# Token norms by one GpSimd power, and the rotary and gate multiplications on VectorE, in a two-layer hybrid encoder

## The chip, the cores and the metric

The kernel runs on one core of one Trainium2 chip. The metric is the device time of one execution in microseconds (us), taken as the median of several executions. One further execution is profiled; the trace and all its views come from that one.

## What is computed

A trunk of two layers works on 512 tokens of width 1024, in float32. Each layer does this, and a last RMSNorm follows:

```python
h = rms_norm(x, g_mix);  z = h @ w_in            # q, k, v, xb, gb
q, k = partial_rope(q), partial_rope(k)          # 16 of 64 columns rotate
o = softmax(q1 k1) - lam * softmax(q2 k2), @ v   # 4 heads
o = rms_norm(o, subln) * (1 - lam_init)          # per head
c = centred_dwconv(xb)                           # 4 taps
for d in (forward, backward):                    # RG-LRU
    r, i = sigmoid(c @ w_r), sigmoid(c @ w_i)
    a = exp(-8 r softplus(-A));  u = c * i * sqrt(1 - a*a);  h_d = scan(a, u)
r = rms_norm((h_f + h_b) * gelu(gb), norm_g)
x += concat(o, r) @ w_out
x += cross_attention(rms_norm(x, g_xq), rms_norm(mem, g_mem))   # 4 heads, 256 memory tokens
x += relu(rms_norm(x, g_mlp) @ w1)**2 @ w2
```

`rms_norm(x, g)` is `x * rsqrt(mean(x*x) + 1e-6) * g`.

## The kernel before

**Layout and products.** The residual x stands transposed, as eight tiles of 128 channels by 512 tokens. Each weight block of 128x1024 is loaded by DMA, split by ScalarE into a rounded part (`whi`) and by VectorE into the remainder (`wlo`), and each product is three matmuls of float32r parts. The results lie in PSUM, in three banks called `mm` and five called `at`; VectorE and ScalarE bring them out.

**Norms.** The factor of a token is not multiplied into x ahead of a product, but into its result. A `Norm` adds up squares; `rstd` sums them over partitions by four matmuls with ones, makes the mean square `ms` (128x4: four token blocks) on VectorE and calls `rsqrt_small`, which builds the reciprocal root by a bit trick and three Newton steps: ten VectorE instructions on 128x4, each needing the one before. Four TensorE transposes (`bcast`) then spread the factor over the partitions. There are 18 such calls: one for each of the three token norms of a layer (six), the last norm, the memory norm, the recurrent norm of each layer (two) and the norm of each attention head (eight, `Head.norm`, where three VectorE instructions make `ms` and one multiplies after).

**Rotary and gates.** `qk_one` takes q or k of one head out of PSUM: a shuffle and a multiplication with `Cr` on VectorE, a multiplication of the shuffled tile with `Sr` on GpSimd, a sum on VectorE, then the split. There are 16 of these. `lru_gates` computes sigmoids for two channel blocks and two directions; the input gate of each is multiplied with the conv's output on GpSimd, 16 in all. GpSimd also does the small zeroing at the edges of the conv's tile `xb` (two columns) and two of the last eight output multiplications.

**Order of the work.** The program is recorded as operations with a key (TensorE time at which they are due, less a lead), and `Plan.schedule` makes one order for all queues: each engine in turn takes the operation that can start first by the plan's own durations, and among those that can start at the same moment the one of smallest key:

```python
            lim = smin + self.LOOK      # LOOK = 0.0
            return min(((k, i, s) for s, k, i in best if s <= lim))
```

An operation becomes ready 0.2 us (`LAT`) after one on another engine, and on VectorE 0.127 us (`OWN`) after one on its own. The durations come from `Plan.cost`. The chip then runs each engine's list strictly in that order, waiting on semaphores. `FILL` and `ORDER` say how much projection, recurrence and memory work is recorded between the 16 attention steps of a layer. All of them are issued from line 412, so the rows are told apart by tile names: `s` is every small column tile, `b` every 128x512 tile, `c_ident` and `c_ones` the constants of the transposes and sums.

Of the kernel before, what the change touches and what calls it, by code (L numbers as in the profile page):

```python
# [11 lines left out]
F32 = mybir.dt.float32  # L12
F32R = mybir.dt.float32r
I32 = mybir.dt.int32
AF = mybir.ActivationFunctionType
ALU = mybir.AluOpType
AX = mybir.AxisListType

P = 128
# [131 lines left out]
class Plan:  # L151
# [43 lines left out]
    def cost(self, eng, m, a, k):  # L195
        out = a[0] if a else k["out"]
        n = 1
        for d in out.shape[1:]:
            n *= d
        if eng == "pe":  # L200
            if m == "transpose":
                return 0.109
            f32 = a[1].root.dtype == F32
            if n < 64:
                return 0.224
            return n * 0.00176 if f32 else max(0.114, n * 0.000456)
        if m == "dma_start":
            return 0.06
        if eng == "act":
            t = 0.093 + n * 0.000833  # L210
            t += 0.093 * sum(isinstance(k.get(x), _View) for x in ("scale", "bias", "accum_out"))
            return t
        if eng == "dve":
            if m == "tensor_reduce":
                n = 512
            if m == "tensor_scalar_mul":
                return 0.066 + n * 0.0007
            ap = m == "scalar_tensor_tensor" and isinstance(a[2], _View)
            return 0.067 + n * 0.00105 + 0.06 * ap
        if eng == "pool":  # L220
            return 0.1 + n * (0.0022 if m != "memset" else 0.001)
        return 0.06
# [192 lines left out]
def trunk(tc, ctx, xT, memT, pos, W, par, outT):  # L415
# [10 lines left out]
    V, A, G, PE, SP = (plan.engine(e) for e in ("dve", "act", "pool", "pe", "sp"))  # L426

    def C(shape, dt, name):
        return plan.tile("c_" + name, shape, dt)

    def R():
        return plan.tile("b", [P, S], F32R)

    def T():
        return plan.tile("b", [P, S], F32)

    def SM(n):
        return plan.tile("s", [P, n], F32)

    def MM():  # L440
        return plan.tile("mm", [P, S], F32)
# [4 lines left out]
    def b(v):  # L446
        return v.bitcast(F32)


    def split(dst_hi, dst_lo, src):  # L450
        A.activation(dst_hi, src, AF.Copy)
        V.tensor_tensor(dst_lo, src, b(dst_hi), op=ALU.subtract)
# [19 lines left out]
    def weight(l, t):  # L472
        raw = pre.pop(t, None) if l == 0 else None
        first = raw is not None
        if raw is None:
            raw = raw_weight(l, t)
        hi = plan.tile("whi", [P, 1024], F32R)
        lo = plan.tile("wlo", [P, 1024], F32R)
        with plan.ahead(SPLIT_AHEAD):
            for cs in (slice(0, 512), slice(512, 1024)) if first else (slice(0, 1024),):  # L480
                split(hi[:, cs], lo[:, cs], raw[:, cs])
        return hi, lo

    def gemm_fm(l, t, xs, out, order=range(KD)):

        hi, lo = weight(l, t)
        for i, k in enumerate(order):
            xh, xl = xs[k]
            wh = hi[:, k * P:(k + 1) * P]
            with plan.group():  # L490
                PE.matmul(out, wh, xh, start=(i == 0), stop=False)
                PE.matmul(out, wh, xl, start=False, stop=False)
                PE.matmul(out, lo[:, k * P:(k + 1) * P], xh, start=False, stop=(i == KD - 1))

    def rsqrt_small(ms, n):

        y = SM(n)
        V.tensor_scalar(y.bitcast(I32), ms.bitcast(I32), -0.5, 1597463007.0,
                        op0=ALU.mult, op1=ALU.add)
        for _ in range(3):  # L500
            t = SM(n)
            V.tensor_tensor(t, y, y, op=ALU.mult)
            V.scalar_tensor_tensor(t, t, -0.5, ms, op0=ALU.mult, op1=ALU.mult)
            V.scalar_tensor_tensor(y, t, 1.5, y, op0=ALU.add, op1=ALU.mult)
        return y

    def bcast(col, ncol, out):
# [17 lines left out]
    def pc(l, name, i):  # L525
        o = l * NPL + PC[name] + i
        return prm[:, o:o + 1]
# [4 lines left out]
                    pattern=[[-1, P]], channel_multiplier=1)  # L532
    ones = C([P, P], F32, "ones")
    G.memset(ones, 1.0)

    class Norm:

# [12 lines left out]
        def rstd(self, width, ncol):  # L550
            st = AT()
            with plan.group():
                for c in range(ncol):
                    cs = slice(c * P, (c + 1) * P)
                    PE.matmul(st[:, c:c + 1], self.acc[:, cs], ones[:, 0:1], start=True, stop=True)
            ms = SM(ncol)
            V.tensor_scalar(ms, st[:, :ncol], 1.0 / width, EPS, op0=ALU.mult, op1=ALU.add)
            return rsqrt_small(ms, ncol)
# [66 lines left out]
    def rope_tables(sn, cs, rt):  # L625

        Ct, St = T(), T()
        G.memset(St, 0.0)
        Cv = Ct.split_free(4, 2, 64)
        Sv = St.split_free(4, 2, 64)  # L630
        rb8 = rt.unsqueeze(2).to_broadcast([P, 4, 8])
        rb48 = rt.unsqueeze(2).to_broadcast([P, 4, 48])
        for j in range(2):
            V.tensor_tensor(Cv[:, :, j, 0:8], cs, rb8, op=ALU.mult)
            V.tensor_copy(Cv[:, :, j, 8:16], Cv[:, :, j, 0:8])
            V.tensor_copy(Cv[:, :, j, 16:64], rb48)
            V.tensor_tensor(Sv[:, :, j, 8:16], sn, rb8, op=ALU.mult)
            V.tensor_scalar_mul(Sv[:, :, j, 0:8], Sv[:, :, j, 8:16], -1.0)
        out = []
        for src, tag in ((Ct, "Cr"), (St, "Sr")):  # L640
            p_ = AT()
            with plan.group():
                for c in range(4):
                    PE.transpose(p_[:, c * P:(c + 1) * P], src[:, c * P:(c + 1) * P], ident)
            dst = plan.tile(tag, [P, S], F32)
            A.activation(dst, p_, AF.Copy)
            out.append(dst)
        return out
# [68 lines left out]
    def lru_gates(l, pr, conv, neg, posi):  # L717

        gh, gl = weight(l, T_G + pr)
        gs = {}  # L720
        for c2 in range(2):
            c = 2 * pr + c2
            cc, ch, cl = conv[c]
            for d in range(2):
                for q in range(2):
                    pm = MM()
                    o = (4 * c2 + 2 * d + q) * P
                    with plan.group():
                        PE.matmul(pm, gh[:, o:o + P], ch, start=True, stop=False)
                        PE.matmul(pm, gh[:, o:o + P], cl, start=False, stop=False)  # L730
                        PE.matmul(pm, gl[:, o:o + P], ch, start=False, stop=True)
                    t = T()
                    A.activation(t, pm, AF.Sigmoid, bias=pc(l, "b_i" if q else "b_r", d * 4 + c))
                    if q:
                        G.tensor_tensor(t, cc, t, op=ALU.mult)
                    gs[c2, d, q] = t
        av = {}
        for c2 in range(2):
            for d in range(2):
                r = gs[c2, d, 0]  # L740
                col = l * 8 + d * 4 + 2 * pr + c2
                a, a2 = T(), T()
                A.activation(a, r, AF.Exp, scale=neg[:, col:col + 1])
                A.activation(r, r, AF.Tanh, scale=posi[:, col:col + 1])
                A.activation(a2, a, AF.Square)
                V.scalar_tensor_tensor(r, a2, 1.0, r, op0=ALU.add, op1=ALU.mult)
                av[c2, d] = a
        return gs, av
# [49 lines left out]
    def qk_one(l, t, xs, Cr, Sr, scale):  # L798
        pm = MM()
        gemm_fm(l, t, xs, pm)  # L800
        sh, q = T(), T()
        V.stream_shuffle(sh, pm, SHUF)
        V.tensor_tensor(q, pm, Cr, op=ALU.mult)
        G.tensor_tensor(sh, sh, Sr, op=ALU.mult)
        V.tensor_tensor(q, q, sh, op=ALU.add)
        hi, lo = R(), R()
        if scale is None:
            split(hi, lo, q)
        else:
            A.activation(hi, q, AF.Copy, scale=scale)  # L810
            V.scalar_tensor_tensor(lo, q, scale, b(hi), op0=ALU.mult, op1=ALU.subtract)
        return hi, lo
# [399 lines left out]
    for l in range(DEPTH):  # L1212
# [8 lines left out]
        Cr, Sr = rope_tables(sn, cs, rt)  # L1221
# [221 lines left out]
```

## Time and profile before

| | us |
|---|---|
| median of 3 runs | 1533.76 (1530.17 to 1539.23) |
| the profiled execution | 1536.88 |
| its span, first to last instruction | 1535.1 |
| TensorE busy | 1476.1 |
| VectorE busy | 1183.5 |
| ScalarE busy | 727.1 |
| GpSimd busy | 54.1 |

The busy times come from the profile of that one execution, and a busy TensorE is not a TensorE at full rate: matmul ends are modelled. The trace was read for its mean granted TensorE clock too, 0.978 of full speed over the span. Layer 0 takes the first half of the span, layer 1 the second; in each, attention and recurrence come first, then cross-attention, then the MLP.

### The profile page before, as it was taken

The numbers are of one execution on the slowest core, as the hardware profiler recorded it, in microseconds if no ns is written. First come the engines' busy times: TensorE is split into PE (matmuls) and PEld (weight loads), VectorE is DVE, ScalarE is ACT, GpSimd is POOL, SyncE is SP. The second block draws the span as 40 slices with busy tenths as digits, with TensorE's granted clock in tenths as the row PEclk, the third lists the DMA queues.
The fourth block names the chain that finished last, engine by engine and source line by source line (L and its number), as shares of the span: only waits on it lengthen the run. The fifth ranks groups of instructions, "written<-read, shape, count | busy, mean of one in ns | idle before, by whom it ended". The sixth has DMA issues, their size and how long they took to land.

```text
span 1535.1 us, 20895 instructions
## 1 busy us (share of the span) xinstructions
PE 1476.1 (96%) x8038; PEld 1242.4 (81%) x8038; DVE 1183.5 (77%) x2107; ACT 727.1 (47%) x1099; POOL 54.1 (4%) x59
## 2 busy tenths in 40 slices
PE   8979999999999999999999799999999999999996
PEld 6757788888889889898977577888888898988985
DVE  7899886655589696979868876865656887969696
ACT  5587664444334343434535875553443433434243
POOL 0031000000000000000001310000000000000000
PEclk9989999999999999999999987999999999999998
DMA  5322342311222323222242213422112323232321
GB/s 194 97 82 78 129 138 82 110 69 56 96 96 83 110 84 122 98 97 97 87 134 81 85 57 110 144 101 96 55 69 82 110 84 107 86 110 83 116 88 58
DMA packets 45107, 148.24 MB, mean 97 GB/s; under 512 B 5584, under 2 KB 5712, under 8 KB 45008
## 3 DMA queue, kind: packets, MB, share of 16 engines
q1 hardware_dynamic: 44864, 146.65, 28.0%
q8 instruction: 63, 1.03, 0.3%
q14 instruction: 36, 0.29, 0.1%
q10 hardware_dynamic: 144, 0.26, 0.0%
HBM read 136.41 MB, written 2.10 MB: 90 GB/s over the span
## 4 chain that ended last, share of the span: by engine, by line
PE 85%; DVE 10%; issue 2%; DMA 1%; ACT 1%; SPq 0%; DVEq 0%; ACTq 0%
PE mm L412 65%; PE at L412 20%; DVE b L412 6%; DVE wlo L412 2%; DVE pt L412 1%; DVE s L412 1%; ACT b L412 1%; DMA b<-b 0%; DVE c_x L412 0%; DMA wraw<-in_W 0%; DMA c_x<-in_xT 0%; DMA wraw<-in_memT 0%; SPq L412 0%; ACT whi L412 0%; ACT Cr L412 0%
## 5 line engine op out<-in xcount | busy, mean ns | idle before, releaser
L412 PE MATMUL mm<-b,whi 128*128 128x512 f32 (+1 forms) x3648 | 991.3, 359 | 13.0 <-ACT b L412 6.2
L412 PEld LDWEIGHTS mm<-b,whi 128*128 128x128 f32 x3648 | 638.5, 190 | 126.3 <-ACT b L412 8.6
L412 PE MATMUL mm<-b,wlo 128*128 128x512 f32 (+1 forms) x1824 | 651.0, 357 | 8.0 <-DVE wlo L412 8.0
L412 ACT ACTIVATE whi<-wraw 128x1024 fp32r<-128x1024 f32 (+1 forms) x223 | 233.7, 1049 | 372.6 <-issue 168.3
L412 PEld LDWEIGHTS mm<-b,wlo 128*128 128x128 f32 x1824 | 345.8, 190 | 64.7 <-DVE wlo L412 10.0
L412 DVE TENSOR_TENSOR wlo<-wraw,whi 128x1024 fp32r<-128x1024 f32 (+1 forms) x223 | 277.1, 1243 | 37.2 <-ACT whi L412 36.9
L412 DVE TENSOR_TENSOR b<-b,b 128x512 fp32r<-128x512 f32 (+3 forms) x374 | 219.2, 602 | 15.6 <-ACT b L412 13.3
L412 ACT ACTIVATE b<-b 128x256 fp32r<-128x256 f32 (+2 forms) x224 | 130.3, 596 | 151.9 <-DVE b L412 151.3
L412 DVE TENSOR_TENSOR c_x<-c_x,mm 128x256 f32<-128x256 f32 (+1 forms) x160 | 73.8, 472 | 73.0 <-PE mm L412 71.6
L412 ACT ACTIVATE whi<-pt 128x1024 fp32r<-128x1024 f32 x64 | 67.9, 1061 | 101.6 <-PE mm L412 75.5
L412 PE MATMUL at<-b,whi 128*128 128x256 f32 x512 | 91.8, 278 | 0.0
L412 DVE TENSOR_TENSOR b<-mm,rb 128x512 f32<-128x512 f32 x72 | 49.5, 687 | 53.2 <-PE mm L412 52.5
L412 PE MATMUL at<-b,b 128*128 128x256 f32 (+1 forms) x320 | 83.9, 371 | 3.1 <-DVE b L412 2.2
L412 ACT ACTIVATE b<-at,s 128x512 f32<-128x512 f32 (+2 forms) x100 | 61.0, 614 | 41.9 <-DVE s L412 41.4
L412 DVE TENSOR_TENSOR wlo<-pt,whi 128x1024 fp32r<-128x1024 f32 x64 | 78.2, 1221 | 0.6 <-ACT whi L412 0.3
L412 DVE TENSOR_REDUCE s<-at 128x1 f32<-128x512 f32 (+1 forms) x80 | 54.4, 688 | 31.3 <-PE at L412 31.3
L412 PEld LDWEIGHTS at<-b,whi 128*128 128x128 f32 x512 | 77.6, 188 | 0.0
L412 PEld LDWEIGHTS at<-b,b 128*128 128x128 f32 x320 | 50.1, 195 | 30.9 <-issue 22.6
L412 PE MATMUL at<-b,wlo 128*128 128x256 f32 x256 | 71.1, 278 | 0.0
L412 PE MATMUL at<-pt,b 128*128 128x256 f32 (+1 forms) x288 | 53.1, 332 | 4.2 <-ACT pt L412 2.9
L412 PEld LDWEIGHTS at<-pt,b 128*128 128x128 f32 x288 | 45.3, 200 | 12.2 <-ACT pt L412 3.9
L412 DVE TENSOR_TENSOR c_x<-c_x,at 128x256 f32<-128x256 f32 x96 | 40.1, 419 | 18.1 <-PE at L412 17.7
(124 smaller groups left out, 1311.4 us busy)
## 6 DMA issues: line engine op xcount, KB each, us to landing
wraw<-in_W SPq DMA_DIRECT2D x249, 512.0 KB, 3.2
b<-b SPq DMA_DIRECT2D x64, 128.0 KB, 2.4
wraw<-in_memT SPq DMA_DIRECT2D x4, 512.0 KB, 3.9
out_T<-b SPq DMA_DIRECT2D x8, 256.0 KB, 2.6
c_x<-in_xT SPq DMA_DIRECT2D x7, 256.0 KB, 5.5
wraw<-in_W SPq DMA_DIRECT2D x6, 256.0 KB, 5.5
c_x<-in_xT ACTq DMA_DIRECT2D x1, 256.0 KB, 3.3
c_prm<-in_par SPq DMA_DIRECT2D x1, 89.0 KB, 3.2
```

The lines of the kernel that those rows point to most:

```text
L412: getattr(self.engines[op.eng], m)(*a, **k)
```

## The change

`rsqrt_small` becomes one GpSimd instruction, `ms` to the power of minus one half, with a constant tile of exponents; the multiplications in `qk_one` and in the input gates go from GpSimd to VectorE; and the plan books every GpSimd operation of up to four columns at 1.0 us. That booking holds for the powers and for the zeroing of two columns alike. The order of all queues is made anew from these durations.

```diff
@@ Plan.cost
+        if eng == "pool" and n <= 4:
+            return 1.0
         if eng == "pool":
             return 0.1 + n * (0.0022 if m != "memset" else 0.001)
@@ rsqrt_small
         y = SM(n)
-        V.tensor_scalar(y.bitcast(I32), ms.bitcast(I32), -0.5, 1597463007.0,
-                        op0=ALU.mult, op1=ALU.add)
-        for _ in range(3):
-            t = SM(n)
-            V.tensor_tensor(t, y, y, op=ALU.mult)
-            V.scalar_tensor_tensor(t, t, -0.5, ms, op0=ALU.mult, op1=ALU.mult)
-            V.scalar_tensor_tensor(y, t, 1.5, y, op0=ALU.add, op1=ALU.mult)
+        G.tensor_tensor(y, ms, mhalf[:, :n], op=ALU.pow)
@@ constants
+    mhalf = C([P, 4], F32, "mhalf")
+    G.memset(mhalf, -0.5)
@@ lru_gates
-                        G.tensor_tensor(t, cc, t, op=ALU.mult)
+                        V.tensor_tensor(t, cc, t, op=ALU.mult)
@@ qk_one
-        G.tensor_tensor(sh, sh, Sr, op=ALU.mult)
+        V.tensor_tensor(sh, sh, Sr, op=ALU.mult)
```

## Rows read from the trace of the kernel before

**Rows 1.** Busy time by stage: window, length, busy by engine (count), clock, DMA.

```profile
80.00:160.00 80.00, 68.95 (x280) 51.03 (x279) 72.42 (x118) 64.94 (x109) 18.04 (x13) 0.89 0.26 80
...
260.00:840.00 580.00, 573.53 (x3212) 491.31 (x3212) 440.53 (x736) 237.12 (x342) 4.88 (x8) 1.00 0.27 93
840.00:960.00 120.00, 104.29 (x460) 80.81 (x459) 92.87 (x175) 85.18 (x137) 19.21 (x13) 0.86 0.28 87
...
sum 1535.00, PE 1476.09 PEld 1242.45 DVE 1183.46 ACT 727.13 POOL 54.11; mean PE 184.51 PEld 155.31 DVE 147.93 ACT 90.89 POOL 6.76
```

**Rows 2.** Timeline of TensorE: start, duration, instruction, idle before and its releaser.

```profile
103.42 1.22 PE L412 MATMUL mm<-b,whi 128*128 128x512 f32 x2 [3.43 <-ACT b L412]
...
109.83 4.72 PE L412 MATMUL at<-b,b 64*128 64x512 f32 x7 [2.19 <-DVE b L412]
...
305.26 0.60 PE L412 MATMUL at<-c_ident,s 128*128 128x128 f32 x4
...
883.77 1.08 PE L412 MATMUL at<-c_ident,s 128*128 128x128 f32 x4 [9.84 <-ACT b L412]
...
1524.72 1.11 PE L412 MATMUL at<-c_ident,s 128*128 128x128 f32 x4 [2.23 <-DVE s L412]
```

**Rows 3.** Groups of VectorE instructions by shape: count | busy, mean ns | idle before.

```profile
L412 DVE TENSOR_TENSOR wlo<-wraw,whi 128x1024 fp32r<-128x1024 f32 x217 | 273.0, 1258 | 36.5 <-ACT whi L412 36.2
...
L412 DVE TENSOR_TENSOR wlo<-pt,whi 128x1024 fp32r<-128x1024 f32 x64 | 78.2, 1221 | 0.6 <-ACT whi L412 0.3
...
L412 DVE SCALAR_TENSOR_TENSOR s<-s,s 128x4 f32<-128x4 f32 x110 | 17.7, 165 | 2.6
...
L412 DVE TENSOR_TENSOR s<-s 128x4 f32<-128x4 f32 x51 | 8.0, 160 | 1.2
...
L412 DVE TENSOR_SCALAR s<-s 128x4 int32<-128x4 int32 x17 | 2.9, 168 | 0.4
```

**Rows 4.** Timeline of VectorE at the last norm.

```profile
1522.72 0.17 DVE L412 TENSOR_SCALAR s<-s 128x4 int32<-128x4 int32 x1
```

**Rows 5.** Groups of GpSimd instructions by shape.

```profile
L412 POOL TENSOR_TENSOR b<-b,b 128x512 f32<-128x512 f32 x16 | 26.6, 1678 | 50.5 <-ACT b L412 50.3
L412 POOL TENSOR_TENSOR b<-b,Sr 128x512 f32<-128x512 f32 x16 | 22.4, 1398 | 768.3 <-ACT Sr L412 647.5 <-DVE b L412 94.2 <-ACT whi L412 26.6
...
L412 POOL MEMSET xb<- 128x2 f32 x16 | 1.0, 98 | 45.7 <-DVE b L412 35.0 <-ACT b L412 10.6
```

**Rows 6.** Timeline of GpSimd: the first multiplication, and two side by side.

```profile
40.80 1.58 POOL L412 TENSOR_TENSOR b<-b,Sr 128x512 f32<-128x512 f32 x1 [38.35 <-ACT Sr L412]
...
104.02 5.21 POOL L412 TENSOR_TENSOR b<-b,b 128x512 f32<-128x512 f32 x2 [7.34 <-ACT b L412]
```

**Rows 7.** Timeline of VectorE in layer 0, while GpSimd multiplies.

```profile
94.88 2.36 DVE L412 SCALAR_TENSOR_TENSOR b<-b,b 128x512 f32<-128x512 f32 x2
...
106.39 3.38 DVE L412 TENSOR_TENSOR b<-b,b 128x512 f32<-128x512 f32 x2
...
125.66 1.20 DVE L412 TENSOR_SCALAR s<-s 128x4 f32<-128x4 f32 x1
...
145.39 1.72 DVE L412 TENSOR_TENSOR wlo<-wraw,whi 128x1024 fp32r<-128x1024 f32 x1
```

**Rows 8.** Timeline of VectorE in layer 1, around the first head's norm.

```profile
870.64 1.27 DVE L412 TENSOR_TENSOR b<-b,b 128x512 f32<-128x512 f32 x2
...
872.96 1.71 DVE L412 TENSOR_TENSOR b<-b,b 128x512 f32<-128x512 f32 x1
874.60 1.22 DVE L412 TENSOR_SCALAR s<-s 128x4 f32<-128x4 f32 x1
...
877.47 0.14 DVE L412 TENSOR_SCALAR s<-s 128x4 int32<-128x4 int32 x1
...
883.46 0.16 DVE L412 TENSOR_TENSOR s<-s,s 128x4 f32<-128x4 f32 x1
```

**Rows 9.** Windows of 10 us behind that norm.

```profile
880.00:890.00 10.00, 6.23 (x15) 3.50 (x15) 8.24 (x24) 9.04 (x19) 0.00 (x0) 0.50 0.13 36
890.00:900.00 10.00, 9.71 (x37) 7.40 (x37) 6.06 (x12) 9.91 (x16) 2.50 (x2) 0.73 0.09 34
```

## The prediction

> **What bounds the kernel now.** I read the busy time by stage first. TensorE is busy for 1476 of 1535 us, and from 260 to 840 us, a stretch of MLP and projections, for 573.5 of 580 at full clock: there VectorE (440.5) has slack and nothing that it saves is worth anything. The two stretches with attention and recurrence are different [rows 1]. From 80 to 160 us VectorE is busy for 72.4 of 80 and TensorE only for 68.9, at a granted clock of 0.89; from 840 to 960 us TensorE lacks 15.7 us, at 0.86. So whatever this change is worth lies in 200 of 1535 us, and at the end, where the last norm has nothing beside it.
>
> Then the timeline of TensorE, to see which wait stands there [rows 2]. In layer 0 the gaps are 3.43 us ahead of 103.4 and 2.19 ahead of 109.8, both behind a full VectorE and ScalarE. In layer 1 there is one gap of 9.84 us, ahead of the four transposes that spread a head's norm (`at<-c_ident,s`). The view names ScalarE as the releaser, but the transposes read `s`, and the last writer of that is VectorE's `s<-s,s` at 883.46 [rows 8]: TensorE's queue stands still for a norm that isn't ready.
>
> **Why that norm is late.** Its three instructions for `ms` end at 875.82 (874.60 + 1.22), the ten of `rsqrt_small` run from 877.47 to 883.4, and the last multiplication at 883.46 [rows 8]. Undisturbed, the ten take 2.0 us: at the last norm the first starts at 1522.72 and TensorE at 1524.72 [rows 2, 4]. In layer 1 they take 7.6 from 875.82, since the plan always takes what can start first (`LOOK` is 0): a small instruction that becomes ready 0.127 us after its predecessor loses to any large one that is ready now, ten times over. The gap is made by the length of the chain in steps, not by its work.
>
> **Part 1, the ten instructions go.** VectorE loses 17 x 10 on 128x4 and 10 on 128x2. By groups: 2.9 (17 bit tricks) + 8.0 (51 squares) + 102/110 of 17.7 (the other 8 belong to the heads' `ms`) = 27.3 us, and the 128x2 call a further 1.6 at the same means, together 28.9 us, 1.6 a norm [rows 3]. Most of it lies beside a busy TensorE. In the norm near 305 us the transposes start without a gap [rows 2], because products of the next stage fill the wait; that cover stays, so norms there count nothing.
>
> **Part 2, the power.** No row shows a power on GpSimd. From below: a GpSimd instruction on 128x2 takes 0.098 us. From above: a multiplication of 512 columns takes 1.40 or 1.68 on average [rows 5], and 2.6 in the slowest pair (5.21 for two) [rows 6]. A power of four columns is near the first in columns and near a whole multiplication in arithmetic per element; I take 1.0, the number the new order is built on, so that a power of that length is waited for by no queue, and keep 0.1 and 2.6 for the range. From VectorE to TensorE the hand-over costs 0.06 (the chain ends at 1524.66); with two hand-overs the power costs 1.13.
>
> On the first power there is one more doubt: whether its code has to be brought in. The first multiplication of GpSimd at 40.80 took 1.58, against 1.40 on average [rows 5, 6], so a first use shows at most 0.2 us here, and the sum goes by that. The Trainium skill (GPSIMD Engine Reference, section 2.1, Instruction dispatch) says that the first call of a freshly loaded GpSimd kernel pays about 6 us that no instruction in the profile shows; by it the forecast would be some 6 us later, and whether a power is such a kernel no row here can tell.
>
> **Part 3, the 32 multiplications move.** VectorE takes a multiplication of this size in 0.69, and 0.60 when another is behind it (two in 1.27) [rows 8]: 32 x 0.60 = 19.2 us more. But GpSimd's multiplications are paid for by VectorE already. While one runs, VectorE instructions with two operands in SBUF stretch: two of 0.69 took 3.38 beside the pair at 104.02 (2.1 too many) [rows 6, 7], a `ms` step of 0.17 took 1.20 [rows 7], and the 217 splits of loaded weights average 1258 ns against 1221 for the 64 splits that fall in stages without GpSimd [rows 3], which alone is 8.0 us. With 2 x 1.05 for two stretched `ms` steps and 1.1, 2.1 and 1.0 for the rows at 94.88, 106.39 and 872.96 [rows 7, 8] I count 14.3 us, at least. So the move costs VectorE some 5 us net in all, and with part 1 VectorE has 24 us less. The queue of GpSimd, emptied of multiplications, never holds up a power.
>
> **Part 4, the booking of 1.0.** The 16 zeroings of `xb`, 0.098 each [rows 5], are booked at 1.0 too. The plan may hold a conv's first tap back by up to 1.8 us (two of them); before it stands the conv's product of 24 matmuls on TensorE, and the tile waits in PSUM for that. I count 0; without that cover it would be 8 x 1.8 = 14 us of plan time, spread over 60 us of a busy TensorE.
>
> **The sum, place by place.**
> - Layer 0, from 94 to 147 us, where VectorE is full: six stretched pieces go, the four shown with 1.1, 2.1, 1.0 and 0.5 too many, and two between them with 0.5 and 0.75 [rows 7], 6.0 together; a head's norm gives 1.6; four gate and three rotary multiplications add 7 x 0.60 = 4.2. Net 3.4 us.
> - Layer 1, the gap: instead of 7.6 us from `ms` to the last multiplication there are 1.13, and 0.7 for one large instruction in hand: 5.8 gained. Ahead of `ms` two stretches go (1.0 and 1.05) and two gate multiplications come (1.2): 0.9 more. Together 6.7 of the 9.84. What is late next are the scores behind the transposes; VectorE was idle between 884 and 902 us for about 7 (it is busy 8.24 and 6.06 of 10 [rows 9]), enough to take them earlier.
> - The last norm: 2.0 becomes 1.13, 0.9 us.
> - All else 0.
>
> That is 11.0 us, and 1536.88 - 11.0 = 1525.9 for the profiled execution. This lies 3.1 above the median of the runs, so the median should be 1523. With powers of 0.1 us it would be 1521.
>
> **Rivals.**
> - *The gap moves instead of closing.* VectorE is the real bound at 870 to 884 us, and TensorE next waits for reductions in place of the norm. For it: VectorE is full there. Against it: the idle time after 884. It costs the 6.7: 1529.5.
> - *The clock comes back too.* Behind the gap the granted clock was 0.50, then 0.73 [rows 9], and in the two stretches 0.89 and 0.86 [rows 1]: 0.11 x 68.95 + 0.14 x 104.29 = 22 us of busy TensorE at the lower level of 1.2 GHz in place of 2.4. If shorter gaps save half, the median is 1512. Against it: a shift of the gap, not its end, would leave the clock as it was.
> - *The power is slower than booked*, and the time longer than before. The new order puts the transposes 0.2 + 1.0 + 0.2 us behind `ms`. TensorE's queue is in order: behind the transposes stand the next products, behind them everything. A power of P stalls it by P + 0.13 - 1.4 at up to 18 places, and the heads' last multiplication holds VectorE's queue likewise. At P = 1.9 that eats the 11 us; at 2.6 it costs 24, and the median is 1547. For it: every multiplication row on GpSimd but the small zeroings is over 1.2. Against it: four columns against 512.
> - *A load of code on the first power.* At the price that rows allow (0.2) nothing changes. The Trainium skill's figure (same page and section) would give 1529, an estimate from it.
> - *The new order makes a wait of its own elsewhere.* All queues are rewritten, and gaps like the 9.84 us arise by order alone: 5 us or so either way, to 1535 or above.
>
> **How the numbers follow.** Chances: the forecast (1518 to 1528) 0.40, the gap that moves 0.22, the clock 0.14, the slow power 0.14, the load 0.05, a wait elsewhere 0.05. A difference under 0.5% (7.7 us, so 1526 to 1541) can hardly be told from none. Faster: four fifths of the forecast, all of the clock, a fifth of the gap's, 0.51. Slower: most of the slow power and half of a wait elsewhere, 0.15. The same: 0.34. The range runs from the clock's 1512, less the 2 of a short power, to 1541, where a power of 2.3 ends.
>
> **What would show it.** Right: no small VectorE chains of ten; powers of about 1 us on GpSimd; the 128x1024 splits of loaded weights at 1221 on average; no gap over 4 us ahead of `c_ident,s` transposes; VectorE busy near 1160. Wrong: GpSimd rows of 2 us or more, with TensorE idle ahead of many transposes; or a gap as long as before in 840 to 960 us, released by a reduction or a scan.

## The result, and the profile after

The changed kernel took 1514.34 us (median of four, 1513.86 to 1515.95), the kernel before 1532.16 on the same chip: a ratio of 0.9877 (over all the runs, so not quite that of the medians), with a 95% interval of 0.9844 to 0.9911. That is 17.8 us between the medians; the profiled execution of the changed kernel took 1514.28 with a span of 1512.5, which is 22.6 less than the span before. The kernel before scatters: beside the experiments it took from 1526.2 us, at a mean granted clock of 0.985, to 1542.6, at 0.973, and its profiled execution lies 4.7 above the median, so up to that much of the 22.6 need not be the change. The forecast was 1523, most likely 1518 to 1528, with a range from 1510 to 1541.

The busy times stand at the head of the profile page of the changed kernel:

```profile
PE 1466.2 (97%) x8038; PEld 1235.8 (82%) x8038; DVE 1159.5 (77%) x1959; ACT 735.3 (49%) x1107; POOL 27.0 (2%) x46
```

VectorE is down from 1183.5 to 1159.5. The same windows of time as in [rows 1], and one of those in [rows 9], show where TensorE stands still now:

```profile
80.00:160.00 80.00, 70.58 (x286) 53.16 (x285) 67.83 (x114) 65.11 (x106) 1.14 (x3) 0.89 0.27 79
...
840.00:960.00 120.00, 115.25 (x592) 91.08 (x593) 108.12 (x183) 101.37 (x160) 3.85 (x3) 0.96 0.35 110
...
880.00:890.00 10.00, 10.00 (x47) 7.72 (x46) 9.97 (x20) 9.97 (x17) 0.00 (x0) 1.00 0.41 119
```

From 840 to 960 us TensorE lacks 4.75 us in place of 15.7, and its granted clock is 0.96 in place of 0.86; from 880 to 890 it is 1.00, where it was 0.50. From 80 to 160 little has changed. The timeline of TensorE in the changed kernel shows, among others, these gaps:

```profile
101.72 1.22 PE L414 MATMUL mm<-b,whi 128*128 128x512 f32 x2 [3.78 <-ACT b L414]
...
109.18 1.56 PE L414 MATMUL at<-pt,b 128*128 128x256 f32 x11 [1.42 <-DVE pt L414]
...
842.16 3.54 PE L414 MATMUL at<-b,b 128*128 128x512 f32 x6 [3.31 <-DMA b<-b]
...
932.96 0.65 PE L414 MATMUL at<-c_ident,s 128*128 128x128 f32 x4 [0.39 <-POOL s L414]
...
1502.10 1.12 PE L414 MATMUL at<-c_ident,s 128*128 128x128 f32 x4 [1.41 <-POOL s L414]
```

The 9.84 us ahead of a head's transposes [rows 2] are gone; there is now a wait of 3.31 us for a DMA, earlier in layer 1. The wait of the last norm is 1.41 in place of 2.23.

The saved time can be placed exactly, because each layer has the same two landmarks on VectorE in every kernel: the first instruction of the norm ahead of attention and recurrence, and that of the norm ahead of cross-attention. In the changed kernel's timeline of VectorE they are:

```profile
31.32 0.16 DVE L414 TENSOR_SCALAR s<-at 128x4 f32<-128x4 f32 x1 [0.45 <-PE at L414]
...
298.17 0.17 DVE L414 TENSOR_SCALAR s<-at 128x4 f32<-128x4 f32 x1 [1.59 <-PE at L414]
...
778.67 0.16 DVE L414 TENSOR_SCALAR s<-at 128x4 f32<-128x4 f32 x1 [3.96 <-PE at L414]
...
1039.35 0.16 DVE L414 TENSOR_SCALAR s<-at 128x4 f32<-128x4 f32 x1 [1.59 <-PE at L414]
```

Before, the same four instructions stood at 32.14, 302.55, 782.80 and 1061.86. So attention and recurrence went from 270.4 to 266.9 us in layer 0, and from 279.1 to 260.7 in layer 1: 3.6 and 18.4 us. The start gave 0.8, the stretch between them cost 0.25, and all behind the last landmark gave 0.1; together that is the 22.6. The question of the study is what made the 18.4, where 6.7 were forecast.

The windows between the two landmarks of layer 1, before and after, split it. TensorE runs the same 1235 matmuls in both:

```profile
782.80:1061.86 279.06, 263.04 (x1235) 206.80 (x1235) 214.53 (x394) 163.90 (x261) 24.09 (x20) 0.94 0.31 100
```

```profile
778.67:1039.35 260.68, 254.49 (x1235) 200.35 (x1235) 209.19 (x349) 171.17 (x268) 8.23 (x10) 0.98 0.34 107
```

TensorE stood still for 16.0 us of this stretch and now does for 6.2, which is 9.8 less. The same matmuls are busy for 254.5 us in place of 263.0, at a granted clock of 0.98 in place of 0.94, which is 8.6 less.

The groups of VectorE and of GpSimd in the changed kernel, by shape:

```profile
L414 DVE TENSOR_TENSOR wlo<-wraw,whi 128x1024 fp32r<-128x1024 f32 x217 | 264.9, 1221 | 42.5 <-ACT whi L414 42.1
...
L414 DVE TENSOR_TENSOR b<-b,Sr 128x512 f32<-128x512 f32 x16 | 10.9, 684 | 0.2
...
L414 DVE TENSOR_SCALAR s<-s 128x4 f32<-128x4 f32 x8 | 1.3, 167 | 0.1
```

```profile
L414 POOL TENSOR_TENSOR s<-s,c_mhalf 128x4 f32<-128x4 f32 x17 | 20.5, 1210 | 1340.7 <-DVE s L414 1337.9 <-PE at L414 2.7
...
L414 POOL TENSOR_TENSOR s<-s,c_mhalf 128x2 f32<-128x2 f32 x1 | 1.2, 1188 | 60.1 <-ACT b L414 60.1
```

The splits of loaded weights, which averaged 1258 ns [rows 3], take 1221. A power takes 1.21 us on average; the timeline of GpSimd shows lengths from about 1 us to about 2:

```profile
31.64 2.09 POOL L414 TENSOR_TENSOR s<-s,c_mhalf 128x4 f32<-128x4 f32 x1 [29.13 <-DVE s L414]
...
121.29 1.01 POOL L414 TENSOR_TENSOR s<-s,c_mhalf 128x4 f32<-128x4 f32 x1 [41.12 <-DVE s L414]
...
778.98 2.09 POOL L414 TENSOR_TENSOR s<-s,c_mhalf 128x4 f32<-128x4 f32 x1 [362.43 <-DVE s L414]
...
926.59 1.01 POOL L414 TENSOR_TENSOR s<-s,c_mhalf 128x4 f32<-128x4 f32 x1 [67.41 <-DVE s L414]
931.07 1.84 POOL L414 TENSOR_TENSOR s<-s,c_mhalf 128x4 f32<-128x4 f32 x1 [3.47 <-DVE s L414]
```

And this is the first head's norm of layer 1 in the timeline of VectorE, the one that [rows 8] show before the change:

```profile
857.53 0.16 DVE L414 TENSOR_TENSOR s<-at,s 128x4 f32<-128x4 f32 x1
857.73 0.16 DVE L414 SCALAR_TENSOR_TENSOR s<-s,s 128x4 f32<-128x4 f32 x1
857.92 0.17 DVE L414 TENSOR_SCALAR s<-s 128x4 f32<-128x4 f32 x1
...
859.21 0.16 DVE L414 TENSOR_TENSOR s<-s,s 128x4 f32<-128x4 f32 x1
...
866.44 2.34 DVE L414 TENSOR_TENSOR_SCAN b<-b,b 128x512 f32<-128x512 f32 x2
...
869.87 1.22 DVE L414 TENSOR_TENSOR_SCAN b<-b,b 128x512 f32<-128x512 f32 x1
```

Two things differ from before. The power saves steps: only one instruction of VectorE, at 859.21, follows the three for `ms`. But the norm also stands in another place: it is over before the scans of the recurrence begin at 866.44. The rows of the kernel before that come ahead of those in [rows 8], in its timeline of VectorE, are:

```profile
865.31 0.16 DVE L412 TENSOR_TENSOR s<-at,s 128x4 f32<-128x4 f32 x1 [1.26 <-PE at L412]
...
865.99 0.15 DVE L412 SCALAR_TENSOR_TENSOR s<-s,s 128x4 f32<-128x4 f32 x1
...
868.39 2.34 DVE L412 TENSOR_TENSOR_SCAN b<-b,b 128x512 f32<-128x512 f32 x2
...
871.83 1.22 DVE L412 TENSOR_TENSOR_SCAN b<-b,b 128x512 f32<-128x512 f32 x1
```

Three scans stand there between the second instruction for `ms` and the third, which is the row at 874.60 [rows 8]. Whether the shorter chain or the other place closed the gap, the trace of the changed kernel can't tell.

### The profile page after: what moved, and what is told of

It reads as the page before. It is cut to its first block, busy times and chain, and to the rows that moved or that the text cites. A ratio compares the mean times of both kernels' runs of the same rounds, so it can differ in the third digit from the quotient of the medians.

```text
span 1512.5 us, 20682 instructions
## 1 busy us (share of the span) xinstructions
PE 1466.2 (97%) x8038; PEld 1235.8 (82%) x8038; DVE 1159.5 (77%) x1959; ACT 735.3 (49%) x1107; POOL 27.0 (2%) x46
## 4 chain that ended last, share of the span: by engine, by line
PE 90%; DVE 5%; ACT 2%; DMA 1%; issue 1%; POOL 0%; SPq 0%; DVEq 0%; POOLq 0%; ACTq 0%
PE mm L414 70%; PE at L414 20%; DVE b L414 2%; DVE wlo L414 2%; ACT b L414 2%; DVE pt L414 1%; ACT L414 1%; POOL s L414 0%; DVE c_x L414 0%; DMA b<-b 0%; ACT whi L414 0%; DMA c_x<-in_xT 0%; DMA wraw<-in_W 0%; DVE s L414 0%; SPq L414 0%
## 5 line engine op out<-in xcount | busy, mean ns | idle before, releaser
L414 DVE TENSOR_TENSOR wlo<-wraw,whi 128x1024 fp32r<-128x1024 f32 (+1 forms) x223 | 269.0, 1207 | 43.2 <-ACT whi L414 42.8
L414 DVE TENSOR_TENSOR b<-b,b 128x512 fp32r<-128x512 f32 (+2 forms) x390 | 225.0, 593 | 11.9 <-ACT b L414 10.3
L414 PE MATMUL at<-b,b 128*128 128x256 f32 (+1 forms) x320 | 80.6, 361 | 3.9 <-DMA b<-b 3.6
L414 DVE TENSOR_TENSOR wlo<-pt,whi 128x1024 fp32r<-128x1024 f32 x64 | 78.1, 1220 | 0.3
L414 DVE TENSOR_TENSOR c_x<-c_x,at 128x256 f32<-128x256 f32 x96 | 40.0, 417 | 18.1 <-PE at L414 17.8
L414 PE MATMUL at<-b,pt 128*128 128x256 f32 x384 | 51.5, 281 | 0.0
L414 PE MATMUL at<-pt,b 128*128 128x256 f32 (+1 forms) x288 | 49.8, 320 | 1.4 <-DVE pt L414 1.4
```

Of the source, the lines that this page charges most:

```text
L414: getattr(self.engines[op.eng], m)(*a, **k)
```

## The experiments

All ratios are to the kernel before, run beside the experiment on the same chip, with 95% intervals. In the edits `V` is VectorE and `G` is GpSimd; each edit is to the kernel that its first line names, and where that isn't the changed kernel, norms are Newton's unless the edit says otherwise.

**The power alone.** The norms and the booking as in the changed kernel, the 32 multiplications still on GpSimd.

```diff
@@ the kernel before
+        if eng == "pool" and n <= 4:
+            return 1.0
...
-        V.tensor_scalar(y.bitcast(I32), ms.bitcast(I32), -0.5, 1597463007.0,
...
+        G.tensor_tensor(y, ms, mhalf[:, :n], op=ALU.pow)
```

> Only the norms change: one GpSimd power instead of ten VectorE instructions, booked at 1.0 us; the rotary and gate multiplications stay on GpSimd. Theory A (the long gap in layer 1 came from a chain of small VectorE steps between which large instructions were taken; the power shortens the chain to one step): most of the 18 us is here, 1515 to 1522 us, and TensorE has no gap over 4 us ahead of a head's transposes. Theory B (VectorE's work is what counts, and GpSimd's multiplications stretch it): VectorE keeps the stretch of 14 us or more and loses 29 us of small work, most of it where it costs nothing; 1526 to 1531 us, and the 128x1024 splits of loaded weights stay near 1258 ns. A further doubt: powers that queue behind multiplications of 1.3 to 2.6 us on GpSimd come late; then TensorE waits at several transposes and the time is nearer to before.

It took 1533.45 against 1535.49: 0.9977 (0.9958 to 0.9997). The gap that the power was to close stayed, in two pieces, in the timeline of TensorE of this run:

```profile
879.34 1.12 PE L414 MATMUL at<-c_ident,s 128*128 128x128 f32 x4 [5.49 <-DVE pt L414]
885.60 2.96 PE L414 MATMUL at<-b,b 128*128 128x512 f32 x4 [2.94 <-ACT b L414]
```

Its timeline of VectorE says why:

```profile
865.92 0.15 DVE L414 SCALAR_TENSOR_TENSOR s<-s,s 128x4 f32<-128x4 f32 x1
...
868.33 2.33 DVE L414 TENSOR_TENSOR_SCAN b<-b,b 128x512 f32<-128x512 f32 x2
...
874.53 0.16 DVE L414 TENSOR_SCALAR s<-s 128x4 f32<-128x4 f32 x1
...
877.94 0.15 DVE L414 TENSOR_TENSOR s<-s,s 128x4 f32<-128x4 f32 x1
```

The second and third instructions for `ms` are still 8.6 us apart, with scans between them. The steps behind them were the smaller part of the delay: in [rows 8] 7.6 us from the end of the third, against 8.5 between the second and the third. The power did shorten those steps, and the wait ahead of the transposes fell from 9.84 to 5.49, but a wait of 2.94 for the scores (`at<-b,b`) opened behind it.

**The moves alone.** Newton's ten instructions stay on VectorE, the 32 multiplications come to it as well.

```diff
@@ the kernel before, lru_gates and qk_one
-                        G.tensor_tensor(t, cc, t, op=ALU.mult)
+                        V.tensor_tensor(t, cc, t, op=ALU.mult)
...
-        G.tensor_tensor(sh, sh, Sr, op=ALU.mult)
+        V.tensor_tensor(sh, sh, Sr, op=ALU.mult)
```

> Only the 32 multiplications change: rotary and gates on VectorE, the norms with their ten VectorE instructions as before. Theory A: the chain of small steps stays and VectorE's queue is no emptier, so the long gap ahead of a head's transposes in layer 1 stays in some form (over 5 us); 1528 to 1535 us. Theory B: the stretch goes (splits near 1221 ns, no small step over 0.3 us) and the time falls by 3 to 7 us, 1526 to 1530.

It took 1514.73: 0.9864 (0.9839 to 0.9889), the whole gain without any power. The head's norm, still with its ten instructions, runs from 856.40 to 860.69 in its timeline of VectorE, ahead of the scans:

```profile
856.40 0.15 DVE L412 TENSOR_TENSOR s<-at,s 128x4 f32<-128x4 f32 x1
...
860.53 0.16 DVE L412 TENSOR_TENSOR s<-s,s 128x4 f32<-128x4 f32 x1
...
865.36 2.34 DVE L412 TENSOR_TENSOR_SCAN b<-b,b 128x512 f32<-128x512 f32 x2
```

**The ten instructions as one unit.** In the kernel before, the plan takes the ten together, booked at 1.94 us, so that nothing can come between them.

```diff
@@ the kernel before, rsqrt_small
+        with plan.group():
...
-        for _ in range(3):
-            t = SM(n)
+            for t in ts:
```

> The kernel before with the same instructions on the same engines, but the plan takes the ten VectorE instructions of a norm as one unit of 1.94 us, so that nothing is put between them. Theory A: this alone closes the long gap in layer 1: the ten run in about 2 us there, and the time falls by 8 to 18 us, to 1515 to 1525. Theory B: VectorE's work is unchanged, so the time stays within 4 us of before.

It took 1538.47: 1.0024 (1.0001 to 1.0047). The ten do run unbroken, from 886.62 to 888.5, but the third instruction for `ms` stands behind the scans at 883.75, and TensorE waits 8.21 us. A short chain behind a late `ms` is not worth the 5.8 us that were forecast for it.

**The changed kernel again**, beside these three:

> The changed kernel itself, on the same chip as the three above: 1512 to 1518 us by any theory. If the effects of the two halves add, its gain is the sum of theirs; if the order made by the plan decides, it need not be.

It took 1516.02: 0.9863 (0.984 to 0.9885). With the power or without it, the moves give the same.

**Order and engine apart.** A move does two things: the plan makes another order, and another engine does the work. The next two runs take one of them each, with Newton's norms in both. In the first, the plan believes that VectorE multiplies, but the instructions go to GpSimd; in the second the other way round.

```diff
@@ the kernel before, where operations are issued
-                getattr(self.engines[op.eng], m)(*a, **k)
+                eng, m = m.split(":") if ":" in m else (op.eng, m)
+                getattr(self.engines[eng], m)(*a, **k)
@@ first kernel, lru_gates and qk_one
-        G.tensor_tensor(sh, sh, Sr, op=ALU.mult)
+        getattr(V, "pool:tensor_tensor")(sh, sh, Sr, op=ALU.mult)
@@ second kernel, lru_gates and qk_one
-        G.tensor_tensor(sh, sh, Sr, op=ALU.mult)
+        getattr(G, "dve:tensor_tensor")(sh, sh, Sr, op=ALU.mult)
```

> The norms as before. The plan books the 32 multiplications on VectorE and makes the order of the moved kernel (1515 us in the run before this), but they are issued on GpSimd. Theory C (GpSimd's multiplications cost time by running beside VectorE: the stretch and their own 1.3 to 2.6 us): the gain is lost, 1528 to 1540 us, with splits of loaded weights back near 1250 ns. Theory D (the order is what gained: with the multiplications on VectorE the plan puts recurrence and attention in another sequence): most of the gain stays, 1514 to 1522.

> The norms as before. The plan books the 32 multiplications on GpSimd and makes the order of the kernel before, but they are issued on VectorE at the same places of the order. Theory C: the gain is here, 1514 to 1522 us. Theory D: no gain, since the order with its long gap in layer 1 is the old one and VectorE gets 19 us more in a place that the plan thinks free: 1528 to 1540, with a gap over 5 us near 880 us.

The new order on the old engine took 1524.41: 0.9935 (0.9907 to 0.9963). The old order on the new engine took 1532.12: 0.9984 (0.9965 to 1.0003). The first has no gap ahead of transposes; in its timeline of VectorE the norm starts at 860.67 and ends before the scans, though the multiplications on GpSimd stretch it:

```profile
860.86 1.05 DVE L413 SCALAR_TENSOR_TENSOR s<-s,s 128x4 f32<-128x4 f32 x1
861.94 1.42 DVE L413 TENSOR_SCALAR s<-s 128x4 f32<-128x4 f32 x2
...
865.64 0.16 DVE L413 TENSOR_TENSOR s<-s,s 128x4 f32<-128x4 f32 x1
...
871.25 2.33 DVE L413 TENSOR_TENSOR_SCAN b<-b,b 128x512 f32<-128x512 f32 x2
```

The second has lost the stretch (its splits of loaded weights average 1220 ns), but the gap is there in full, in its timeline of TensorE:

```profile
879.92 1.09 PE L413 MATMUL at<-c_ident,s 128*128 128x128 f32 x4 [9.53 <-ACT b L413]
```

**Gates alone, rotary alone.** Newton's norms, and half of the moves each.

```diff
@@ first kernel, lru_gates
-                        G.tensor_tensor(t, cc, t, op=ALU.mult)
+                        V.tensor_tensor(t, cc, t, op=ALU.mult)
@@ second kernel, qk_one
-        G.tensor_tensor(sh, sh, Sr, op=ALU.mult)
+        V.tensor_tensor(sh, sh, Sr, op=ALU.mult)
```

> The norms and the rotary multiplications as before, only the 16 gate multiplications on VectorE, planned and issued there. In layer 1 the gain of the moved kernel was 18 us between the first and the second token norm, where the gate pairs run. Theory C: the two pairs at 104 and 871 us, the slowest ones (2.5 us each), were the stretch that mattered, and this gives the larger part, 1518 to 1525. Theory D: any change of the plan's durations in the recurrence makes another order; the result is either near 1515 or near before, with nothing in between.

> The norms and the gate multiplications as before, only the 16 rotary multiplications on VectorE, planned and issued there. Theory C: the smaller part of the gain, 1526 to 1531 us, since a rotary multiplication stretches a split by 0.5 to 0.8 us and most of those splits are ahead of their use; both parts together (with the run above) should make the 20 us of the moved kernel. Theory D: near 1515 or near before, independent of how many multiplications are moved.

The gates alone took 1525.55: 0.9949 (0.9928 to 0.9969), with a gap of 8.64 us ahead of transposes at 879.56. The rotary alone took 1519.58: 0.9906 (0.987 to 0.9942), with no such gap: the norm runs from 859.51 to 863.60, the scans start at 868.28. So it is the rotary's multiplication, planned on VectorE, that brings the norm ahead of the scans. What the gates alone save, with that gap still there, was not taken apart. Their gains add up (0.51 + 0.94 = 1.45%, where both together gave 1.36).

**The norm's whole work as one unit.** If the place of the third instruction for `ms` is the cause, the kernel before should lose the gap by planning all that VectorE does for a norm (three for `ms`, ten, one) as one unit. The same was put on the kernel with the moves alone.

```diff
@@ the norms of the kernel before, and of that with the moves alone
+            with plan.group():
...
                 V.tensor_scalar(ms, ms, EPS, None, op0=ALU.add)
                 y = rsqrt_small(ms, 4)
                 V.tensor_tensor(y, y, r1, op=ALU.mult)
```

> The kernel before, same engines and instructions, but the plan takes a norm's VectorE work as one unit: of a head the three instructions for the mean square, the ten and the last multiplication. In the runs so far every order with the gap ahead of a head's transposes in layer 1 had the third of the three instructions behind the scans of the recurrence, and every order without it had the whole norm ahead of them. Theory E (the gap is this: a norm torn apart by the scans, with TensorE's queue standing behind its transposes): the gap goes, layer 1 gains 8 to 15 us, total 1519 to 1527. Theory F (the gap is only where a stretch that VectorE fills shows; take it here and it shows elsewhere): the gap ahead of the transposes goes but another of similar length stands in 840 to 960 us, total 1529 to 1537.

> The 32 multiplications on VectorE, norms on VectorE as ten instructions, planned as one unit with the three ahead and the one behind. The norm of layer 1 is ahead of the scans in the moved order already, so both theories E and F say little change from the moved kernel (1515 us): 1510 to 1520. If the units help at other norms, it is below the changed kernel's time.

On the kernel before it took 1531.3: 0.9984 (0.9966 to 1.0002). The unit runs unbroken from 877.05 to 879.78, ahead of the scans at 880.91, and the wait ahead of the transposes is 0.70 us. New waits stand behind it, in its timeline of TensorE:

```profile
879.93 0.62 PE L416 MATMUL at<-c_ident,s 128*128 128x128 f32 x4 [0.70 <-DVE s L416]
...
881.90 0.73 PE L416 MATMUL mm<-b,whi 128*128 128x512 f32 x2 [1.35 <-ACT b L416]
...
887.84 1.22 PE L416 MATMUL mm<-b,whi 128*128 128x512 f32 x2 [2.72 <-DVE b L416]
...
893.87 1.22 PE L416 MATMUL mm<-b,whi 128*128 128x512 f32 x2 [4.38 <-ACT b L416]
```

By the landmarks its layer 1 is 8.9 us shorter than before (270.2), and its layer 0 8.3 us longer (278.7). The gap closes, but the time is that of theory F (1529 to 1537) and not that of theory E (1519 to 1527): the three waits behind it make 8.5 us, and the order of everything else moves by as much. On the kernel with the moves it took 1525.18, 0.9948 (0.9929 to 0.9968), which is 10 us more than the moves alone by the medians; its layer 0 takes 272.4 in place of 266.7.

**The changed kernel, with the three for `ms` as one unit.**

```diff
@@ the changed kernel, Head.norm
+            with plan.group():
...
                 V.tensor_scalar(ms, ms, EPS, None, op0=ALU.add)
```

> The changed kernel with the three instructions of a head's mean square planned as one unit ahead of the power. Only the last three steps can be torn apart in the changed kernel and its trace shows none that is, so 1511 to 1518 us by any theory; a larger change would say that orders alone scatter by more than that.

It took 1514.25: 0.9875 (0.9851 to 0.9899), the same as the changed kernel: there they are together anyway.

**Each power twice.** The second power repeats the first into another tile; the pair is booked at 1.0, as the one was.

```diff
@@ the changed kernel, Plan.cost and rsqrt_small
-            return 1.0
+            return 0.5 if m == "tensor_tensor" else 1.0
...
+        with plan.group():
+            G.tensor_tensor(y0, ms, mhalf[:, :n], op=ALU.pow)
...
             G.tensor_tensor(y, ms, mhalf[:, :n], op=ALU.pow)
```

> The changed kernel, but each norm issues its power twice on GpSimd (the first result is unused) while the plan books the pair at 1.0 us, so every power is 1.0 us later than planned. This prices the rival of a slow power. If TensorE's queue stands at each of 18 norms until the power is there: 18 x (2.02 + 0.13 - 1.4) = 13 us more, about 1528. If most of the 18 are covered by products already issued or by slack in the order: 2 to 5 us, 1516 to 1520.

It took 1520.68: 0.9921 (0.9898 to 0.9943), about 6 us more than the changed kernel, or 0.35 us for each of the 18 powers of 1 us that were added. The order is the planned one, so most places have work in hand for part of a late power. One place where it doesn't reach, in the timeline of TensorE (the row at 932.96 with 0.39 in the changed kernel):

```profile
939.32 0.65 PE L414 MATMUL at<-c_ident,s 128*128 128x128 f32 x4 [1.36 <-POOL s L414]
```

No run beat the changed kernel beyond its interval.

**How long TensorE stands still in layer 1, run by run.** Between the two landmarks of layer 1 every run has the same 1235 matmuls. The length of the stretch less TensorE's busy time is the time for which it stands still, and most of the clock's scatter stays out of it.

| run | TensorE idle, us |
|---|---|
| the kernel before | 16.0 |
| the power alone | 15.6 |
| ten instructions as one unit | 18.1 |
| old order, issued on VectorE | 16.1 |
| gates alone | 14.1 |
| whole norm as one unit | 13.6 |
| new order, issued on GpSimd | 8.5 |
| rotary alone | 8.4 |
| moves alone | 6.2 |
| moves alone, whole norm as one unit | 7.7 |
| the changed kernel | 6.2 |
| the changed kernel again | 6.1 |
| the changed kernel, three for `ms` as one unit | 6.1 |
| the changed kernel, each power twice | 7.3 |

The runs fall into two groups: those whose plan has the rotary on GpSimd (13.6 or more) and those whose plan has it on VectorE (8.5 or less).

## Why the prediction was right and wrong, step by step

**The direction was right, and the time lies inside the range, though below the 1518 to 1528 of the forecast; the reason was not right.** Of the 11.0 us, 8.3 were put down to the norms (5.8 in the gap, 1.6 in layer 0, 0.9 at the end). The power alone gave 0.23%, about 3.5 us with an interval from 0.5 to 6.4, and on top of the moves nothing that can be measured. The moves, credited with 2.7 net, gave all of it (1535.49 to 1514.73, 20.8 us).

**The step that failed** is "the gap is made by the length of the chain in steps, not by its work", and with it the 5.8 us. In [rows 8] the third instruction for `ms` starts at 874.60, 8.5 us behind the end of the second (865.99 + 0.15). The prediction started its clock at 875.82, where that instruction ends, and counted what came after. In every run with the gap (before, the power alone, ten as a unit, old order on VectorE, gates alone) scans stand between the second and the third; in every run in which the rotary is planned on VectorE the norm ends ahead of the scans and there is no such gap. Shortening the steps behind `ms` isn't enough: one power in their place left 5.49 + 2.94 us, one unbroken unit 8.21. Taking away the stretch isn't either: the old order on VectorE left 9.53. Keeping the scans out of the norm is enough for this gap: as a whole unit it left 0.70. It isn't enough for the time: waits of 8.5 us stood behind it, TensorE was idle for 13.6 us of layer 1 where it had been for 16.0, and the run was no faster clear of noise (0.9984, up to 1.0002). In that run, and in part with the power alone (2.94 us ahead of the scores), the rival "the gap moves instead of closing" came true, though not to reductions. What the runs show in place of the failed step is that the order of VectorE's whole list, with the rotary planned on it, took the idle time away (16.0 to 8.5 us by the order alone, 6.2 with the engine), and the late norm was one place where the old order showed.

**Layer 1, 6.7 forecast, 18.4 measured.** By the windows between the landmarks, 9.8 of it is idle time of TensorE and 8.6 is the clock, for the same matmuls. Of the idle time, the 9.84 and a later gap of 2.90 (before an `at<-pt,b` at 933.32), which the prediction did not list, are gone, and a wait of 3.31 for a DMA has come. So the rival "the clock comes back too" came true in layer 1, where [rows 9] had shown 0.50 and 0.73 behind the gap; in layer 0 the busy time fell by only 1.7 us (258.8 to 257.1 between its landmarks). Together the 10.3 us are near the 11 of that rival, but its size is read from one execution before that was slower than its median, and part of it may be scatter. Its time, 1512, was the nearest to the measured 1514.3 of all that were written down, at a chance of 0.14. That nearness is in part luck: the 1512 still holds the 11.0 us of the forecast, of which 8.3 were put down to the norms.

**Layer 0, 3.4 forecast, 3.6 measured.** The waits at 101.72 and 109.18 are still there, as expected of a full VectorE. But the agreement of the sum is no proof of its terms: 1.6 of it was a head's norm, and the moves alone, without that, have a layer 0 of 266.7 us, as short as the changed kernel's 266.9.

**The costs of instructions were right.** A power of 1.0 is 1.01 where nothing disturbs it; VectorE's busy time fell by 24.0, as summed; the splits came to 1221, which is 8.1 us where 8.0 were forecast; the eight third steps for `ms` fell from 429 to 167 ns on average; the moved multiplications take 0.684. The wait of the last norm shrank by 0.8 where 0.9 were forecast, though all behind 1061.86 is only 0.1 shorter. What the booking of the zeroings does to the order was not run by itself; the moves alone, with the old booking, gained as much as the changed kernel.

**What the moves are worth** splits in two. The order alone gave 0.65%, the engine alone 0.16% with an interval that takes in no change, both together 1.36%. On top of the new order the engine is therefore worth another 0.7%, some 11 us. That the stretch and the 1.4 to 1.6 us of a GpSimd multiplication stand on the path there, and that in the old order the gap swallows what they give, is a reading that no run takes apart. The prediction priced the engine and put the order under "a wait elsewhere", at "5 us or so either way".

**The other rivals.** In the changed kernel the gap did not move to reductions. The slow power was overpriced: its rule (a power of P stalls by P + 0.13 - 1.4) gives 13 us for powers that end 1 us later at all 18 places, and the doubled power cost 6. On the code load: the first power, at 31.64, took 2.09 us and started 0.16 after `ms` ended; the one at 778.98, in mid-run, took 2.09 as well. The Trainium skill's 6 us for the first call of a freshly loaded kernel (GPSIMD Engine Reference, section 2.1, Instruction dispatch) are therefore not seen here: this execution does not show such a price for a power. Whether an earlier execution of the kernel had already paid it, no run here shows.

**What stays open.** Why the plan, with the rotary on VectorE, brings the norm's statistics ahead of the scans is not settled: that it does is shown by the eight profiles with that plan, the decision itself was not followed through the plan. Edits that change only the plan moved the time by up to 10 us (10 us by the medians from the moves alone to the same with units, 13 by the ratios; 8.9 less and 8.3 more in the two layers of the first run with them), so part of the 0.65% may belong to this particular list and to no rule. Bookings of the power other than 1.0 were not run.

## What to carry to other kernels

When a queue is in order and its order is made from costs, look at each late result for the instruction that is late and at what stands ahead of it in its queue, from the first step of the chain, not from where the chain looks long. A change that moves work between engines changes the list too: run the new order on the old engine and the old order on the new one before either is given the credit. And price the clock with the gap, where rows behind the gap show it at a lower level.

## What the runs showed of the hardware

The stretch between VectorE and GpSimd goes both ways. Beside a multiplication on GpSimd a VectorE instruction of 0.17 us took 1.20 [rows 7]. A power is itself held when VectorE was first, as this row of the changed kernel's timeline of VectorE, beside the power at 778.98, shows:

```profile
778.98 1.23 DVE L414 TENSOR_TENSOR wlo<-wraw,whi 128x1024 fp32r<-128x1024 f32 x1
```

The split keeps its usual length and ends at 780.21, and the power ends at 781.07, 0.86 behind it. The powers at 31.64 and 931.07 end 0.88 and 0.87 us behind the splits beside them (31.63 to 32.85 and 930.82 to 932.04). The other way round nothing is held: beside the power at 926.59, which lasts to 927.60, VectorE's timeline has this row.

```profile
927.08 1.23 DVE L414 TENSOR_TENSOR wlo<-wraw,whi 128x1024 fp32r<-128x1024 f32 x1 [0.56 <-ACT whi L414]
```

The split starts 0.49 us behind the power and takes no longer than usual. Two products of 512 columns that start inside powers (at 121.89 and 858.60) keep their 0.68 as well. The Trainium skill (SBUF — State Buffer, SBUF: two separate sides) says that a GpSimd instruction and a VectorE instruction with two inputs in SBUF, or in a two-port performance mode, exclude each other for the whole instruction, and whichever starts first holds the port. The three rows in which the split came first agree with it; the three in which the power came first do not, so a power of four columns doesn't keep VectorE out for its whole 1.01 us. The 1.20 above is of an instruction with one input in SBUF, though the prediction counts it among those with two; whether it ran in a two-port mode, no row shows.

A power of four columns takes 1.01 us undisturbed, while the last two products of 512 columns on GpSimd take 2.50 together (`b<-b,rb`, at 1503.92 in the changed kernel), 1.25 each. So four columns of powers cost nearly as much as 512 of products. The two columns of the memory norm took 1.19, but beside VectorE instructions with two inputs (at 182.33 and 182.94); what they take undisturbed, no row shows.
